# Where three context projections run during an attention block: all after the last heads, or spread behind the groups of heads

## The chip, the cores and the metric

One core of one Trainium2 chip runs the whole program in one launch. The metric is device microseconds (us) of that core for one execution, the median of several runs. TensorE (PE) multiplies, VectorE (DVE) and ScalarE (ACT) do elementwise work, GpSimd (POOL) does a few masks, and SyncE (SP) issues every DMA.

## What is computed

The reference is a chain of two blocks over 256 tokens of width 1024. Block 1 has two layers: in layer 0 a SwiGLU network, an attention mixer and a second SwiGLU network; in layer 1 the same with an RWKV-7 mixer. Block 2 attends over the tokens and a second sequence, the context. What bears on the change is the end of layer 0's mixer, and the projections of the context that block 2 needs.

```python
# block 1, layer 0: four stick-breaking heads, and three groups of four dilated heads
outs, lses = [], []
for g, (window, dilation) in enumerate(DIL_PATTERNS):
    o, l = dilated_window_attention(q[:, :, sl], k[:, :, sl], v[:, :, sl], ...)
    outs.append(o); lses.append(l)
alpha = jax.nn.softmax(jnp.stack(lses, axis=0), axis=0)
out_b = jnp.sum(alpha[..., None] * jnp.stack(outs, axis=0), axis=0)
merged = jnp.concatenate([out_a, out_b], axis=-1)
return merged @ w_out

# block 2, layer 0: one projection of the normalized context, cut in sections
z = h @ p['w_in']
z_glu, z_qa, z_kva, z_kr, z_gq, z_gk, z_gv, z_gate = split_sections(z)
y = a * jax.nn.sigmoid(g)                         # a, g: the halves of z_glu
gates = jax.nn.sigmoid(z_gate + p['b_gate'])
```

The three groups' outputs are weighted with a softmax over the groups, so nothing of `out_b` can be weighted before the third group has its denominators. The context's sections depend on the context alone, so they can be computed at any time before block 2.

## The kernel before

**Products.** Each float32 weight chunk of 512 KB (two 128-row pieces of 512 columns) is loaded (`wraw`, 4 buffers), rounded on ACT to `whi` (L73, 3 buffers), and DVE writes the remainder `wlo` (L74, 3 buffers). A product is then three matmuls: high by high, high by low, low by high. `lin` (L89) streams 512 weight columns past the tokens' 128-column pieces: 12 matmuls a chunk, lines L85, L86, L87. `linT` and `linT_units` (L104, L133) hold the weights and stream 256 tokens: 24 matmuls a chunk, lines L151, L152, L153. Results land in the PSUM buffers `mm`, of which there are three.

**The mixer.** `attn_` (L443) projects and runs the stick-breaking heads, then loops over the three groups g of dilated heads: a projection of values for groups 1 and 2 once, a projection of q and k (`lin`, 4 chunks, two `mm` buffers), and `dil_heads` (L574). That normalizes q and k (squares L579, sums L580, a chain of small DVE operations to L584, the scaling L588), transposes them (L592), and for two token tiles and two parities forms logits (L610), adds the bias (L612), takes the maximum (L614), the exponential with its sum (L618), transposes it (L623) and multiplies by the values (L629). The maxima and sums `md` are transposed (L635) and copied into `stat` (L639, L641).

**The combination.** Behind the loop stand the maximum over groups (L490, L491), a difference and an exponential (L493, L494), products and sums (L496 to L498), a reciprocal (L499), the weights `e` (L500), six transposes of them (L504), their copy `wg` (L506), and for each group and token tile the weighting of `og` (L511), two transposes (L514) and a copy or addition into `ob` (L518, L520). `split` (L449) rounds `ob` to `mh` (L450) and writes the remainder `ml` (L451); then the output projection `w_aout` runs (`lin` at L526), and per half of the columns its result is added to x (L529), which is transposed for the next network (`late_half`, L227 to L231).

**Context steps.** The context was normalized earlier. A generator (`ctx_steps`, L1773) yields its projections one by one; `ctx_ahead(n)` (L1762) runs n of them. The order is in `CO`; the first three are the two halves of the glu section and the first half of gate 0:

```python
CO = [('glu', 0, i) for i in range(2)] + [('gate', br, i) for br in (0, 1, 2) for i in range(2)] + ...
```

Each of the three is 4 chunks by 24 matmuls (96) and two `mm` buffers; ACT and DVE turn the result into `keep` (tanh L1802 and product L1803 for glu, four tanh L1798 for a gate), and SP stores it (L1804, L1799). The calls in the mixer, whose counts the change sets:

```python
        for g in range(3):
            ...
            og.append(s.dil_heads(g, ps, vg, stat, fill))
            ...
            s.ctx_ahead(CE[g])
        ...
        split(ob, 2, 2)
        fill(FA[3])
        s.ctx_ahead(CE[3])
        mf = ...
        for cg in range(2):
            ps = s.lin(wout, cg, mf)
```

**What sets the order.** The framework's scheduler lays down one fixed order per engine when the program is built: an operation that is ready goes ahead of a waiting one, and among ready ones the one written earlier goes first. So a step that is written behind group g starts in the gaps of group g and of what follows it. On the chip each engine takes its own list in order.

Of the kernel before, what the change touches and what calls it, by code (L numbers as in the profile page):

```python
# [360 lines left out]

CE = (0,0,0,3)
FA = (0,(0,0,0),0,0)


class Attn:
# [74 lines left out]
    def attn_(s, x, hi, lo, fill, post, win, wout):  # L443
# [31 lines left out]
        for g in range(3):  # L475
# [8 lines left out]
            if SB == g + 1:  # L484
                s.sb_heads(qT, kT, v, split, fill)
            s.ctx_ahead(CE[g])

# [34 lines left out]
        fill(FA[3])  # L522
        s.ctx_ahead(CE[3])
        mf = [lambda k, t=t: (mh[:, k, t * P:(t + 1) * P], ml[:, k, t * P:(t + 1) * P]) for t in range(2)]
# [1721 lines left out]
```

## Time and profile before

| | |
|---|---|
| median of 3 runs | 2669.93 us (2665.99 to 2678.96) |
| the profiled execution | 2672.3 us, of which its span is 2670.6 us |
| busy share of the span | PE 96%, weight loads 85%, DVE 77%, ACT 52%, POOL 1% |
| mean granted TensorE clock | 0.983 of full speed |
| DMA | 482.35 MB, 181 GB/s |

The mixer's groups lie between 268 and 345 us of the span, the combination between 344 and 364 us, the output projection up to 380 us. In the rows, PE is the matmuls and PEld the weight loads, which overlap them; a time in brackets is how long an engine was idle before the row, and behind the arrow is what ended that. A matmul's own duration is longer than the distance to the next one, since matmuls are pipelined: the start-to-start distance is what one costs.

### The profile page before, as it was taken

The page shows a single profiled execution, that of the slowest core. Times are in us where ns is not written, and L with a number is a line of the kernel's source. Part 1 is how long each engine was busy: PE and PEld are TensorE (multiplying, and loading weights), DVE is VectorE, ACT ScalarE, POOL GpSimd, SP SyncE. Part 2 cuts the span into 40 slices and gives each one's busy share as a digit, 9 for nine tenths or more (in the row PEclk, how much of TensorE's full clock was granted, in tenths as well). Part 3 has the DMA queues.
Part 4 walks back from the last instruction along what each step waited for, and adds up shares of the span by engine and source line. Part 5 has one row for each costly group of instructions (what it writes and reads, how often), then busy time and mean ns, then how long its engine had stood idle before and what let it go on. Part 6 is the DMA issues. An engine that isn't in the chain of part 4 may idle for free.

```text
span 2670.6 us, 49859 instructions
## 1 busy us (share of the span) xinstructions
PE 2574.6 (96%) x20144; PEld 2265.3 (85%) x20144; DVE 2045.9 (77%) x3371; ACT 1387.4 (52%) x2155; POOL 27.7 (1%) x22
## 2 busy tenths in 40 slices
PE   8999999999988999999989999979999999999999
PEld 8986799999865787798876999867979978889997
DVE  7965689679987744796574888789887856997885
ACT  4455554444435323444466565566566645755663
POOL 0000000000001100000000000000000000000000
PEclk9998999999999999999989999989999999999999
DMA  7765368667655355577554565540545555325554
GB/s 262 254 220 164 126 221 270 203 232 248 222 190 195 111 162 170 193 258 230 187 174 142 181 193 183 180 136 25 172 152 179 182 158 170 123 76 174 171 185 152
DMA packets 153136, 482.35 MB, mean 181 GB/s; under 512 B 23709, under 2 KB 38817, under 8 KB 151881
## 3 DMA queue, kind: packets, MB, share of 16 engines
q1 hardware_dynamic: 152906, 479.17, 54.9%
q8 instruction: 158, 2.59, 0.4%
q14 instruction: 72, 0.59, 0.1%
HBM read 466.61 MB, written 12.49 MB: 179 GB/s over the span
## 4 chain that ended last, share of the span: by engine, by line
PE 81%; DVE 10%; ACT 3%; DMA 3%; issue 3%; SPq 0%; POOL 0%; DVEq 0%; ACTq 0%
PE mm L153 9%; PE mm L151 8%; PE mm L152 8%; PE mm L86 8%; PE mm L87 8%; PE mm L85 8%; PE tp L151 6%; PE tp L153 5%; PE tp L152 5%; DVE wlo L74 3%; PE at L1709 2%; PE at L1720 2%; PE tp L1716 1%; DMA mraw<-in_w_modT 1%; PE mm L755 1%
## 5 line engine op out<-in xcount | busy, mean ns | idle before, releaser
L73 ACT CAST whi<-wraw 128x1024 fp32r<-128x1024 f32 (+1 forms) x742 | 770.2, 1040 | 828.3 <-PE mm L87 303.4
L74 DVE TENSOR_TENSOR wlo<-wraw,whi 128x1024 fp32r<-128x1024 f32 (+1 forms) x742 | 897.2, 1211 | 368.9 <-ACT whi L73 359.5
L153 PE MATMUL mm<-hhi,wlo 128*128 128x256 f32 x1872 | 533.1, 286 | 9.9 <-DVE wlo L74 9.7
L151 PE MATMUL mm<-hhi,whi 128*128 128x256 f32 x1872 | 535.0, 286 | 4.8 <-ACT whi L73 2.3
L152 PE MATMUL mm<-hlo,whi 128*128 128x256 f32 x1872 | 532.2, 285 | 0.0
L151 PE MATMUL tp<-hhi,whi 128*128 128x256 f32 x1360 | 390.4, 287 | 0.6 <-ACT R L324 0.2
L153 PE MATMUL tp<-hhi,wlo 128*128 128x256 f32 x1360 | 383.6, 282 | 0.4 <-issue 0.4
L152 PE MATMUL tp<-hlo,whi 128*128 128x256 f32 x1360 | 383.7, 282 | 0.0
L153 PEld LDWEIGHTS mm<-hhi,wlo 128*128 128x128 f32 x1872 | 355.3, 190 | 17.0 <-DVE wlo L74 13.8
L151 PEld LDWEIGHTS mm<-hhi,whi 128*128 128x128 f32 x1872 | 356.9, 191 | 8.2 <-ACT whi L73 3.2
L152 PEld LDWEIGHTS mm<-hlo,whi 128*128 128x128 f32 x1872 | 356.7, 191 | 3.8 <-issue 2.5
L151 PEld LDWEIGHTS tp<-hhi,whi 128*128 128x128 f32 x1360 | 257.8, 190 | 4.6 <-issue 1.3
L153 PEld LDWEIGHTS tp<-hhi,wlo 128*128 128x128 f32 x1360 | 257.7, 190 | 0.6 <-issue 0.6
L152 PEld LDWEIGHTS tp<-hlo,whi 128*128 128x128 f32 x1360 | 257.6, 189 | 0.0
L85 PE MATMUL mm<-whi,fh 128*128 128x512 f32 x616 | 243.2, 395 | 0.7 <-ACT fh L1905 0.5
L86 PE MATMUL mm<-wlo,fh 128*128 128x512 f32 x616 | 242.8, 395 | 0.8 <-DVE wlo L74 0.8
L87 PE MATMUL mm<-whi,fl 128*128 128x512 f32 x616 | 242.8, 395 | 0.0
L86 PE MATMUL mm<-wlo,hhi 128*128 128x512 f32 (+1 forms) x448 | 183.9, 411 | 8.2 <-DVE wlo L74 8.1
L85 PE MATMUL mm<-whi,hhi 128*128 128x512 f32 (+1 forms) x448 | 182.0, 409 | 6.7 <-ACT whi L73 6.7
L87 PE MATMUL mm<-whi,hlo 128*128 128x512 f32 (+1 forms) x448 | 184.4, 412 | 1.8 <-DVE hlo L812 1.8
L1309 DVE CUSTOM_DVE_ANT_0 mjunk<-mraw,crow 128x1024 f32<-128x1024 f32 x112 | 136.8, 1221 | 8.3 <-DMA mraw<-in_w_modT 8.1
L85 PEld LDWEIGHTS mm<-whi,fh 128*128 128x128 f32 x616 | 116.6, 189 | 29.3 <-ACT fh L1905 1.7
(537 smaller groups left out, 3916.0 us busy)
## 6 DMA issues: line engine op xcount, KB each, us to landing
wraw<-in_wgu SPq DMA_DIRECT2D x176, 512.0 KB
wraw<-in_w_up SPq DMA_DIRECT2D x132, 512.0 KB
wraw<-in_w_in SPq DMA_DIRECT2D x124, 512.0 KB
wraw<-in_wd SPq DMA_DIRECT2D x88, 512.0 KB
wraw<-in_w_down SPq DMA_DIRECT2D x66, 512.0 KB
mraw<-in_w_modT SPq DMA_DIRECT2D x64, 512.0 KB
wraw<-in_w_mod SPq DMA_DIRECT2D x32, 512.0 KB
wraw<-in_w_attn SPq DMA_DIRECT2D x24, 512.0 KB
```

Of the source, the lines that this page charges most:

```text
L73: a = nc.scalar.copy(out=hi, in_=raw)
L74: v = nc.vector.tensor_tensor(out=lo, in0=raw, in1=hi, op=ALU.subtract)
L85: s.pinned(mm(ps, lhsT=xh, rhs=wh, start=start, stop=False), pin)
L86: mm(ps, lhsT=xh, rhs=wl, start=False, stop=False)
L87: mm(ps, lhsT=xl, rhs=wh, start=False, stop=stop)
L151: s.pinned(mm(ps, lhsT=wh, rhs=xh, start=start, stop=False), pin)
L152: mm(ps, lhsT=wh, rhs=xl, start=False, stop=False)
L153: mm(ps, lhsT=wl, rhs=xh, start=False, stop=stop)
L755: ins = s.nc.tensor.matmul(*a, **k)
L1309: V.tensor_tensor_reduce(out=t, in0=raw, in1=s.crow[:, c], scale=1.0, scalar=0.0, op0=ALU.mult, op1=ALU.add, accum_out=m[:, k, c:c + 1])
L1709: T.matmul(lg[:, j * S:(j + 1) * S], lhsT=q(hs[par])[:, t * P:(t + 1) * P], rhs=k, start=i == 0, stop=i == len(ks) - 1)
L1720: T.matmul(o[64 * par:64 * par + 64, pr], lhsT=kvs[j // 2][1](4 * g + 2 * pr + par, j % 2), rhs=pTs[par][:, j], start=j == 0, stop=j == nt ...
```

## The change

```diff
-CE = (0,0,0,3)
+CE = (1,1,0,1)
```

`CE[g]` is the number of context steps that are called behind group g, and `CE[3]` the number called behind the combination, ahead of the output projection. Before, all three steps stand at the end. After, the first half of glu stands behind group 0, the second behind group 1, and the half gate alone at the end. No instruction is added or removed: PE has 15,170 rows in the listing of its order on both sides.

The first place is PE in group 0 of the dilated heads, at the two batches of transposes of the normalized q and k (L592) and the first logits (L610). The minus rows belong to the projection of the values of groups 1 and 2 (`lin`), the plus rows to the first glu step.

```order
 L592 MATMUL tp<-ident,qk 128x128 x4
-L85 MATMUL mm<-whi,hhi 128x512
+L151 MATMUL mm<-hhi,whi 128x256
+L152 MATMUL mm<-hlo,whi 128x256
 L592 MATMUL tp<-ident,qk 128x128 x4
-L86 MATMUL mm<-wlo,hhi 128x512
-L87 MATMUL mm<-whi,hlo 128x512
+L153 MATMUL mm<-hhi,wlo 128x256
+L151 MATMUL mm<-hhi,whi 128x256
+L152 MATMUL mm<-hlo,whi 128x256
+L153 MATMUL mm<-hhi,wlo 128x256
 L610 MATMUL at<-kT,qT 128x128 x2
```

The gaps of the heads are filled on both sides: with three matmuls of 512 columns before, with six of 256 columns after. The values' projection moves behind the step, and with it the two projections of q and k that follow.

The second place is PE around the transposes of the group weights (L504). Before, the third step's matmuls stand ahead of them and behind them:

```order
L153 MATMUL mm<-hhi,wlo 128x256
L151 MATMUL mm<-hhi,whi 128x256
L504 MATMUL tp<-ident,e 128x4 x6
L152 MATMUL mm<-hlo,whi 128x256
L153 MATMUL mm<-hhi,wlo 128x256
```

After, from the last group's last logits to the output projection:

```order
L623 MATMUL tp<-ident,L 128x128 x2
L635 MATMUL tp<-ident,md 4x128
L629 MATMUL at<-v_3086,pT 128x64 x2
L504 MATMUL tp<-ident,e 128x4 x6
L514 MATMUL tp<-ident,og 128x128 x12
L85 MATMUL mm<-whi,mh 128x512
L86 MATMUL mm<-wlo,mh 128x512
```

Before, 140 matmuls of the steps stand between the last L635 and the first matmul of the output projection. After, none does: the last step's 96 are laid into the third group, and 18 of the output projection's 48 matmuls (those that need only the stick-breaking heads) stand ahead of the last L635.

The third place is DVE in the combination, from the copies of the maxima and sums on; the minus rows were there before only.

```order
 L639 COPY stat<-tp 4x2x128 x2
 L491 TENSOR_TENSOR M<-M,stat 4x256
-L74 TENSOR_TENSOR wlo<-wraw,whi 128x1024
 L493 TENSOR_TENSOR e<-stat,M 4x768
-L74 TENSOR_TENSOR wlo<-wraw,whi 128x1024
 L496 TENSOR_TENSOR f<-e,stat 4x768
 L497 TENSOR_TENSOR M<-f 4x256
 L498 TENSOR_TENSOR M<-M,f 4x256
-L74 TENSOR_TENSOR wlo<-wraw,whi 128x1024
 L499 RECIPROCAL M<-M 4x256
-L1803 SCALAR_TENSOR_TENSOR keep<-keep,mm 128x512
 L500 TENSOR_TENSOR e<-e,M 4x768
```

The conversions of the steps' weights and the second `keep` are gone from between the combination's operations.

## Rows read from the trace of the kernel before

**Rows 1.** The page: the chain that ended last, by engine, and the two conversions.

```profile
PE 81%; DVE 10%; ACT 3%; DMA 3%; issue 3%; SPq 0%; POOL 0%; DVEq 0%; ACTq 0%
L73 ACT CAST whi<-wraw 128x1024 fp32r<-128x1024 f32 (+1 forms) x742 | 770.2, 1040 | 828.3 <-PE mm L87 303.4
```

**Rows 2.** Busy time by stretch (busy us and instructions): group 0 of heads, then the combination.

```profile
core 0: us, PE busy (x) PEld busy (x) DVE busy (x) ACT busy (x) POOL busy (x), PEclk, DMA share, GB/s
268.00:305.90 37.90, 36.64 (x180) 28.20 (x179) 25.76 (x53) 18.30 (x36) 0.00 (x0) 1.00 0.38 126
...
345.40:363.70 18.30, 18.27 (x153) 17.91 (x153) 16.63 (x33) 7.70 (x10) 0.00 (x0) 1.00 0.48 155
```

**Rows 3.** Timeline of PE in groups 0 and 1: start, duration, line, idle before.

```profile
297.18 0.39 PE L85 MATMUL mm<-whi,hhi 128*128 128x512 f32 x1
297.41 0.39 PE L86 MATMUL mm<-wlo,hhi 128*128 128x512 f32 x1
...
305.93 0.63 PE L592 MATMUL tp<-ident,qk 128*128 128x128 f32 x4 [0.61 <-DVE qk L588]
```

**Rows 4.** Timeline of PE in the combination.

```profile
344.02 0.38 PE L635 MATMUL tp<-ident,md 128*4 128x128 f32 x2
...
346.00 0.28 PE L151 MATMUL mm<-hhi,whi 128*128 128x256 f32 x1
346.12 0.28 PE L152 MATMUL mm<-hlo,whi 128*128 128x256 f32 x1
...
355.70 0.76 PE L504 MATMUL tp<-ident,e 4*128 4x4 f32 x6
...
363.71 0.39 PE L85 MATMUL mm<-whi,mh 128*128 128x512 f32 x1
```

**Rows 5.** Timeline of DVE in the combination.

```profile
344.44 0.74 DVE L639 COPY stat<-tp 4x256 f32<-4x256 f32 x2 [0.47 <-PE tp L635]
345.11 0.40 DVE L491 TENSOR_TENSOR M<-M,stat 4x256 f32<-4x256 f32 x1
...
346.58 0.94 DVE L493 TENSOR_TENSOR e<-stat,M 4x768 f32<-4x768 f32 x1
...
350.39 0.41 DVE L497 TENSOR_TENSOR M<-f 4x256 f32<-4x256 f32 x1
...
352.31 1.73 DVE L499 RECIPROCAL M<-M 4x256 f32<-4x256 f32 x1
...
354.52 0.93 DVE L500 TENSOR_TENSOR e<-e,M 4x768 f32<-4x768 f32 x1
...
361.73 1.22 DVE L74 TENSOR_TENSOR wlo<-wraw,whi 128x1024 fp32r<-128x1024 f32 x1
362.86 0.48 DVE L520 TENSOR_TENSOR ob<-tp,ob 128x128 f32<-128x128 f32 x2
```

**Rows 6.** Timeline of ACT in the combination.

```profile
348.14 0.84 ACT L494 ACTIVATE e<-e 4x768 f32<-4x768 f32 x1
...
364.75 0.61 ACT L450 CAST mh<-ob 128x512 fp32r<-128x512 f32 x1
```

**Rows 7.** Another idle stretch of PE, in layer 1: its timeline.

```profile
762.57 1.17 PE L85 MATMUL mm<-whi,hhi 128*128 128x512 f32 x2 [3.77 <-ACT whi L73]
768.21 0.80 PE L86 MATMUL mm<-wlo,hhi 128*128 128x512 f32 x1 [4.48 <-DVE wlo L74]
768.81 0.63 PE L87 MATMUL mm<-whi,hlo 128*128 128x512 f32 x1
769.23 0.63 PE L85 MATMUL mm<-whi,hhi 128*128 128x512 f32 x1
...
772.65 0.51 PE L85 MATMUL mm<-whi,hhi 128*128 128x512 f32 x1
```

**Rows 8.** Busy time by stretch, same columns as rows 2, inside that idle stretch.

```profile
760.00:762.00 2.00, 0.00 (x0) 0.00 (x0) 1.88 (x6) 1.42 (x3) 0.00 (x0) 1.00 0.87 352
764.00:766.00 2.00, 0.00 (x0) 0.00 (x0) 2.00 (x6) 0.34 (x1) 0.00 (x0) 0.50 0.93 369
```

## The prediction

> **What bounds the kernel now.** The first view is the chain of work that ended last: TensorE holds 81% of it [rows 1]. So the question is not how much work there is, which the change leaves alone, but whether PE is left without work anywhere. The second view is the busy time by stretch: from group 0 of the heads on, PE is busy 36.64 of 37.90 us, and in the combination 18.27 of 18.30 us, at the full granted clock [rows 2]. Since busy time hides how tightly matmuls follow each other, the third view is PE's timeline. In group 0's gaps, matmuls of 512 columns start 0.23 us apart [rows 3]; in the combination, those of 256 columns start 0.12 us apart, more exactly 0.118 on average over a run of them [rows 4]. Both are back to back. The gaps of the heads are thus closed already, by the projections that come next; the combination is closed by the context steps. The fourth view, DVE's timeline of the combination, shows why it needs them: one operation waits for the other from the copies at 344.44 to the last addition at 362.86 [rows 5].
>
> **The change part by part.** The moved steps cost PE the same wherever they stand: 2 x 96 matmuls by 0.118 us = 22.7 us. Behind groups 0 and 1 they push the projections back by that much and take over their role as filler. The rows of the order show the gaps filled one for one, so the time there is worth nothing: 0 us gained. The projections fill the next gaps in turn, and so the shortage arrives at the end. There, 140 step matmuls stood between the last L635 and the output projection, 140 x 0.118 = 16.5 us. None is left, and the 18 early matmuls of the output projection stand ahead of that point too.
>
> What the end takes without filler is the length of the chain. Part one runs from the last L635 to the weights' transposes L504. From L635 at 344.02 to L491 at 345.11 is 1.1 us [rows 4, 5]. Then come L491 0.40, L493 0.94, the exponential 0.84 [rows 5, 6], L496 as long as L493, 0.94, L497 and L498 0.41 each, L499 1.73, L500 0.93 [rows 5]: 6.6 us; nine handovers at some 0.04 us, as from the end of L635 at 344.40 to L639 at 344.44 [rows 4, 5], 0.4. Sum 8.1 us, against the 11.7 us that it took between 344.02 and 355.70 [rows 4], because the weight conversions that stood in between are gone. Part two runs from L504 at 355.70 to the end of the last addition, 362.86 + 0.48 = 363.34; less the conversion of 1.22 us at 361.73 that stood in it [rows 4, 5], 6.4 us. Then the rounding of `ob`, 0.61 us [rows 6], and a handover. The sum is 8.1 + 6.4 + 0.7 = 15.2 us. In it PE has work of its own: before, 363.71 - 344.02 = 19.7 us held 16.5 us of steps, so 3.2 us. **PE stands idle 15.2 - 3.2 = 12.0 us.** Its bounds: 8.2 us if a quarter of the 15.2 us overlapped, which their dependence speaks against, and 16.5 us if the chain took the 19.7 us that it took before.
>
> **Waits in the third group.** Before, groups 0 and 1 each left PE idle for some 0.6 us ahead of their transposes [rows 3], and group 2 did not, since its projection was ready early. Now its projection ends just ahead, and the wait comes a third time: 0.6 us. Its last exponentials stand behind a conversion of 1.04 us on ACT [rows 1]; that is between 0 and 1.04 us, and I take 0.6, since 12 filler matmuls of 0.23 us stand beside it. Together 1.2 us.
>
> **The clock.** In layer 1, PE stands idle from 758.80 to 768.21 but for two matmuls [rows 7]. The granted clock is still 1.00 (2.4 GHz) from 760 to 762, and 0.50 (1.2 GHz) from 764 to 766 [rows 8]. After the restart, 512-column matmuls start 0.42 to 0.43 us apart until 772.65: ten starts in 4.44 us [rows 7], where 0.23 us each would make 2.3 [rows 3]. That is 2.1 us, and I take it for the restart behind the combination, whose 15.2 us hold only 3.2 us of PE work. The transposes L504 and L514 fall into the slow time: 0.6 us, an estimate from the same doubling of some 1.2 us of their work. Bounds: 0 if the clock holds, 4.8 us if it stays low twice as long behind the restart. Taken: 2.7 us.
>
> A rule speaks to the same point. The Trainium skill (Perfetto Trace Analysis, Matmul Optimizations) says that TensorE's power follows its use, and that matmuls should therefore be issued back to back in batches. The trace of layer 1 agrees, with 10 matmuls at 0.43 us behind its gap.
>
> **Queues and buffers.** Each glu step also brings an ACT tanh, a DVE product and a store to its new place. SP takes its list in order, so the weight loads behind a store wait until `keep` is written. DMA engines are 38% busy in group 0 [rows 2] and four chunks are loaded ahead, so I put this at 0; without that cover each of the two stores could hold one chunk, 12 x 0.23 = 2.8 us, or 5.6 us in all. The three `mm` buffers are passed on as they were between projections: 0. Nothing behind the attention is reordered in a way that costs PE.
>
> **Sum.** 12.0 + 1.2 + 2.7 = 15.9, say 16 us. Against the profiled execution, 2672.3 becomes 2688.3 us. That execution lies 2.4 us above the median of the runs, so for a median I say 2669.9 + 16 = **2686 us**.
>
> **Rivals.**
> - *The clock holds.* The transposes L504 and L514 break the idle time in two, and the granted clock may never fall. For it: the two breaks. Against it: in layer 1 two lone matmuls did not keep the clock up [rows 7, 8]. It gives 16 - 2.7 = 13 us, 2683 us, right at the edge of what can be told.
> - *Not slower: the heads had room.* If the matmuls in group 0's gaps are limited by something else than streaming, the steps slip in for nothing there. It would take place from 268 to 306: weight loads fill 28.20 of 37.90 us, so up to 9.7 us of the steps could vanish, and the end would need less of the work it loses. It gives 2669.9 - 9.7 = 2660 us. It decides from the point at which the start-to-start distance in the gaps exceeds 0.23 us; rows 3 show 0.23, which is what it is everywhere in the dense stretches. The Trainium skill (Perfetto Trace Analysis, Identifying the Most-Contended Engine) has a rule that would say so: judge TensorE's headroom by the weight loads' share, not by its busy time. By that share there is 26% of headroom in group 0 and 2% in the combination.
> - *A late restart.* The next network's first chunks are converted behind the combination instead of inside it. If two of them come late, PE waits for two roundings of 1.04 us and two remainders of 1.22 us more [rows 1, 5], 4.5 us: 2690.5 us. Against it: 30 matmuls of the output projection lie between.
> - *The chain is shorter than added up*, at its lower bound of 8.2 us idle, with no waits and no clock loss: 2678 us.
>
> That the change does nothing is excluded by the order of PE, where the step matmuls are gone from the end.
>
> **How the numbers follow.** The forecast has 0.58, the clock that holds 0.15, the late restart 0.14, the shorter chain 0.06, room in the heads 0.07. About 0.5%, 13.3 us, is what a measurement of this kernel can tell from no change. Slower by more: nine tenths of the forecast's case less what the runs' spread of several us takes away from a middle that lies 2.7 us above the edge, a third of the case in which the clock holds, and the late restart: 0.45 + 0.05 + 0.13 = 0.63. Within: the rest of these, the shorter chain and nearly all of the room, 0.34. Faster: 0.03. The range runs from 2675 us, below the shorter chain's value by a few us of spread, to 2696 us, the late restart with the 5.6 us of held loads; it leaves out the room in the heads and little else.
>
> **What would show it.** In the profile after: the stretches of groups 0 and 1 as long as their matmuls ask for, with 256-column matmuls 0.12 us apart in the gaps; between the last L635 and the first matmul of the output projection about 15 us with some 12 us of PE idle, ended by L500, L511 and L450; a granted clock of 0.50 at the end of it and some ten matmuls at 0.43 us behind; everything after shifted by 14 to 18 us. The prediction is wrong if that stretch holds less than 8 us of idle, if the clock stays at 1.00, or if the heads' stretch gets shorter than the work moved into and out of it explains.

## The result, and the profile after

| | before | after |
|---|---|---|
| median | 2670.72 us (2665.85 to 2678.96, 9 runs) | 2685.99 us (2682.55 to 2693.96, 9 runs) |
| ratio | | 1.0061, 95% interval 1.0048 to 1.0074 |
| the profiled execution, its span | 2672.3 us, 2670.6 us | 2682.97 us, 2681.3 us |

The changed kernel is 15.3 us slower, against a forecast of 16; the interval is 12.8 to 19.8 us. In its profile nothing about the amount of work has changed: PE has 20,144 matmuls on both sides and is busy 96% of the span as before, DVE 76%, ACT 52%, and the conversion L73 still takes 1040 ns each [rows 1]. (The page's chain that ended last covers only a third of the span this time, so its shares aren't compared.) What has changed is one place. Here is PE's timeline of the changed kernel from the end of the third group to the output projection: start, duration, line, tiles, count, and in brackets how long PE was idle before and what ended that.

```profile
343.40 0.30 PE L592 MATMUL tp<-ident,qk 128*128 128x128 f32 x1 [0.58 <-DVE qk L588]
...
361.54 0.27 PE L635 MATMUL tp<-ident,md 128*4 128x128 f32 x1
362.16 0.66 PE L629 MATMUL at<-v,pT 128*128 128x64 f32 x4 [0.35 <-ACT pT L625]
369.55 0.81 PE L504 MATMUL tp<-ident,e 4*128 4x4 f32 x6 [6.73 <-DVE e L500]
371.18 1.09 PE L514 MATMUL tp<-ident,og 128*128 128x128 f32 x4 [0.82 <-DVE og L511]
372.49 1.42 PE L514 MATMUL tp<-ident,og 128*128 128x128 f32 x4 [0.22 <-DVE ob L518]
374.10 0.69 PE L514 MATMUL tp<-ident,og 128*128 128x128 f32 x2 [0.19 <-DVE og L511]
375.70 0.69 PE L514 MATMUL tp<-ident,og 128*128 128x128 f32 x2 [0.91 <-DVE og L511]
377.62 0.80 PE L85 MATMUL mm<-whi,mh 128*128 128x512 f32 x1 [1.23 <-ACT mh L450]
378.21 0.63 PE L86 MATMUL mm<-wlo,mh 128*128 128x512 f32 x1
378.64 0.63 PE L85 MATMUL mm<-whi,mh 128*128 128x512 f32 x1
...
380.77 0.89 PE L87 MATMUL mm<-whi,ml 128*128 128x512 f32 x2
381.50 0.39 PE L85 MATMUL mm<-whi,mh 128*128 128x512 f32 x1
```

Between the last L635 and the first matmul behind the roundings there is little but waits: 0.35 + 6.73 + 0.82 + 0.22 + 0.19 + 0.91 + 1.23 = 10.45 us of listed idle time in 16.1 us. Before, that stretch had no listed wait, with step matmuls 0.12 us apart [rows 4]. DVE's and ACT's timelines show why: the links follow each other within some 0.04 us, and PE is the one that waits.

```profile
361.85 0.74 DVE L639 COPY stat<-tp 4x256 f32<-4x256 f32 x2
362.52 0.40 DVE L491 TENSOR_TENSOR M<-M,stat 4x256 f32<-4x256 f32 x1
362.95 0.95 DVE L493 TENSOR_TENSOR e<-stat,M 4x768 f32<-4x768 f32 x1
364.81 0.95 DVE L496 TENSOR_TENSOR f<-e,stat 4x768 f32<-4x768 f32 x1 [0.91 <-ACT e L494]
...
366.69 1.74 DVE L499 RECIPROCAL M<-M 4x256 f32<-4x256 f32 x1
368.46 0.94 DVE L500 TENSOR_TENSOR e<-e,M 4x768 f32<-4x768 f32 x1
```

```profile
363.93 0.84 ACT L494 ACTIVATE e<-e 4x768 f32<-4x768 f32 x1 [0.71 <-DVE e L493]
376.94 0.62 ACT L450 CAST mh<-ob 128x512 fp32r<-128x512 f32 x1 [12.17 <-DVE ob L520]
```

The durations are those of before [rows 5, 6]; what is gone is the weight conversion that stood among them. The busy time by stretch of the changed kernel (the columns of rows 2) gives the clock: 1.00 ahead of the hole, 0.50 at its end, 1.00 again behind the restart.

```profile
359.00:361.00 2.00, 2.00 (x10) 1.09 (x9) 1.45 (x4) 1.51 (x4) 0.00 (x0) 1.00 0.27 43
364.00:366.00 2.00, 0.00 (x0) 0.00 (x0) 1.16 (x2) 0.78 (x1) 0.00 (x0) 0.56 0.28 113
376.00:378.00 2.00, 0.77 (x3) 0.39 (x2) 0.89 (x3) 0.62 (x1) 0.00 (x0) 0.50 0.00 0
382.00:384.00 2.00, 2.00 (x14) 1.52 (x13) 0.96 (x3) 1.84 (x4) 0.00 (x0) 1.00 0.00 0
```

**Where the time went.** Totals of this kernel scatter by over 10 us, so I compare one stretch in the profiles: from the first L592 of group 0 to the first matmul of the next network (L151 behind the output projection). It holds the same work in both kernels, but for one exchange at its start: in after, 36 step matmuls (4.2 us) stand ahead of it, and the 18 of 512 columns that they pushed (4.2 us) in it. I call it *the stretch*: 273.29 to 375.80 us before, 268.10 to 387.54 us after, that is 102.5 against 119.4 us, **16.9 us longer**. Its parts:

- From the first L592 to the last L635 (before: 344.13 us, the second of the two in the row at 344.02): 70.8 us before, 93.4 after, 22.6 more. The 140 step matmuls from the end (16.5 us at 0.118; for 36 of them, the 18 of that exchange stand in this part) and 18 of the output projection (4.2 us at 0.233) came in, 20.7 us; 1.9 us are lost, 0.9 of them in listed waits.
- From the last L635 to the roundings: 19.6 us before, 16.1 after. Without its 16.5 us of steps, PE's own work there was 3.1 us before and is the same now, so 13.0 us are lost.
- From there to the network: 12.1 us before with 48 matmuls of the output projection, 9.9 after with 30. The 18 that are missing are worth 4.2 us and only 2.2 us were saved: 2.0 us are lost, the half clock.

Each of these comes from one profile. How far that can be trusted shows in the first part, which other kernels below have in the same order: it took 70.8 to 70.9 us in four (before, runs 3, 6 and 11) and 93.4 to 93.6 us in four (after, runs 2, 5 and 8). The clock's part is less steady, by about 1 us in run 5.

The profiled executions differ by only 10.7 us in total, less than the stretch and less than the medians. The difference lies ahead of the change, where both kernels execute the same instructions. There the clock stood at half in the profile of before, and not in that of after; first of before, then of after:

```profile
216.00:228.00 12.00, 12.00 (x41) 7.84 (x40) 2.73 (x8) 3.20 (x10) 0.00 (x0) 0.57 0.43 144
256.00:262.00 6.00, 5.25 (x16) 4.08 (x16) 4.41 (x7) 4.26 (x5) 2.15 (x4) 0.72 0.36 107
```

```profile
216.00:228.00 12.00, 12.00 (x59) 8.72 (x59) 3.95 (x9) 4.35 (x12) 0.00 (x0) 1.00 0.55 175
256.00:262.00 6.00, 5.79 (x31) 3.20 (x30) 3.17 (x5) 2.89 (x6) 2.76 (x4) 1.00 0.48 151
```

That is why after reaches its first L592 5.2 us earlier. It isn't a gift of the change: of the eleven experiments below, six have this low clock in their profile and five don't, with the same instructions there. So: -5.2 + 16.9 + 1.6 in the network behind + some -2.6 spread over the other 2100 us = 10.7 us.

### The profile page after: what moved, and what is told of

Same layout as the page of the kernel before. It is cut to its first block, busy times and chain, and to the rows that moved or that the text cites. A ratio compares the mean times of both kernels' runs of the same rounds, so it can differ in the third digit from the quotient of the medians.

```text
span 2681.3 us, 49861 instructions
## 1 busy us (share of the span) xinstructions
PE 2575.0 (96%) x20144; PEld 2264.4 (84%) x20144; DVE 2046.0 (76%) x3371; ACT 1386.2 (52%) x2155; POOL 27.7 (1%) x22
## 5 line engine op out<-in xcount | busy, mean ns | idle before, releaser
L73 ACT CAST whi<-wraw 128x1024 fp32r<-128x1024 f32 (+1 forms) x742 | 769.4, 1040 | 807.6 <-PE mm L87 310.4
L74 DVE TENSOR_TENSOR wlo<-wraw,whi 128x1024 fp32r<-128x1024 f32 (+1 forms) x742 | 896.1, 1210 | 370.7 <-ACT whi L73 359.7
L151 PE MATMUL mm<-hhi,whi 128*128 128x256 f32 x1872 | 535.7, 286 | 5.1 <-ACT whi L73 2.5
L151 PE MATMUL tp<-hhi,whi 128*128 128x256 f32 x1360 | 390.0, 287 | 0.5 <-ACT R L324 0.2
L151 PEld LDWEIGHTS mm<-hhi,whi 128*128 128x128 f32 x1872 | 357.5, 191 | 9.0 <-ACT whi L73 3.4
L151 PEld LDWEIGHTS tp<-hhi,whi 128*128 128x128 f32 x1360 | 257.6, 189 | 4.4 <-issue 1.0
```

Source lines behind the costliest of these rows:

```text
L73: a = nc.scalar.copy(out=hi, in_=raw)
L74: v = nc.vector.tensor_tensor(out=lo, in0=raw, in1=hi, op=ALU.subtract)
L151: s.pinned(mm(ps, lhsT=wh, rhs=xh, start=start, stop=False), pin)
```

## The experiments

Theory A: the time is lost where PE runs out of work at the end, because the chain there is bare. Theory B, the rival: a step costs by standing behind a group of heads (more waits, more buffers, more queues), whatever is left at the end. The size of the clock's part is a question of its own.

**1. One step behind group 0, two at the end.**

```diff
-CE = (1,1,0,1)
+CE = (1,0,0,2)
```

> One step behind the first group of heads, two at the end. Theory A (the time is lost only where PE runs out of work in the combination): in PE's order 58 step matmuls and 14 of the output projection now stand between the last L635 and L504, 6.8 + 3.3 = 10 us, which covers part one of the chain (8.1 us); 4 of the output projection, 0.9 us, and PE's own 2.3 us are all that stands in part two (7.1 us). So 3.9 us idle there and next to none in part one; with up to 1 us of waits in the groups +4 to +5 us against before, 2675 to 2676 us, and the granted clock stays at 1.00 or falls for a microsecond or two only. Theory B (a step costs by standing behind a group of heads, 15.3 / 2 each, whatever is left at the end): +7.6 us, 2678 us, with the loss in the heads' stretch and not in the combination. The places of the idle time tell them apart better than the total.

Measured: 2678.06 us, ratio to before 1.0021 (1.0009 to 1.0034), that is +5.6 us. The stretch is 108.9 us, +6.3. Its waits are where A put them: none ahead of L504, and the rest in part two.

```profile
360.26 0.73 PE L504 MATMUL tp<-ident,e 4*128 4x4 f32 x6
...
361.95 0.62 PE L514 MATMUL tp<-ident,og 128*128 128x128 f32 x4
362.98 0.44 PE L514 MATMUL tp<-ident,og 128*128 128x128 f32 x2 [0.41 <-DVE ob L518]
364.33 0.77 PE L514 MATMUL tp<-ident,og 128*128 128x128 f32 x4 [0.92 <-DVE og L511]
365.40 0.44 PE L514 MATMUL tp<-ident,og 128*128 128x128 f32 x2 [0.30 <-DVE ob L520]
367.07 0.50 PE L85 MATMUL mm<-whi,mh 128*128 128x512 f32 x1 [1.23 <-ACT mh L450]
...
367.87 0.39 PE L86 MATMUL mm<-wlo,mh 128*128 128x512 f32 x1
368.10 0.57 PE L85 MATMUL mm<-whi,mh 128*128 128x512 f32 x1
368.47 0.63 PE L87 MATMUL mm<-whi,ml 128*128 128x512 f32 x1
```

2.86 us of waits, where 3.9 were expected. But the clock cost more than expected: it fell when the output projection was already running, and from 368.10 us on eight starts in a row are 0.37 to 0.43 us apart, some 1.5 us. The total alone can't tell A from B here; the places speak for A.

**2 and 3. The hole filled again, with the two steps left behind the heads.** Run 2 and its partner, run 3, which takes the same five steps early but all at the end:

```diff
-CE = (1,1,0,1)
+CE = (1,1,0,3)
```

```diff
-CE = (0,0,0,3)
+CE = (0,0,0,5)
```

> The two steps of the change stay behind the first two groups, and three steps, the fourth and fifth of the list among them, stand at the end, so that the end has its full filler again (more than 110 step matmuls behind the last L635). Theory A: the combination has no idle time and the clock stays at 1.00 there; the time is that of five steps at the end (the next run) within 2 us. Theory B: it is slower than that run by 15 us, as after is slower than before.

> None behind the heads, five steps at the end: the partner of the run before, with the same work taken early. Both theories: the combination as in the kernel before, no idle time. What the two additional steps, 2 x 11.3 = 22.7 us of PE ahead of the network, give back behind it is not known from the attention: all of it where they were executed at the cost of PE's time later, nothing if they stood in gaps there. So between 0 and +22.7 us against before; my estimate is +5 us.

Measured: 2684.84 us, 1.0038 (1.0024 to 1.0053), and 2681.97 us, 1.0036 (1.0022 to 1.0049). The stretches are 126.9 and 125.2 us (both with 22.7 us of additional steps): the two steps behind the heads cost **1.8 us**, of which 1.0 in listed waits, and not 15. (The medians are 2.9 us apart, for 2 expected; their scatter is larger than that.) From the last L635 to the output projection run 2 has no listed wait, and its clock over the combination is 1.00:

```profile
366.00:388.00 22.00, 21.90 (x183) 21.42 (x184) 19.36 (x36) 11.08 (x19) 0.00 (x0) 1.00 0.49 163
```

So B is out. Of the 22.7 us that two more steps take early, run 3 keeps 9.6 us as a loss (2672.9 x 0.0036); in its profile, where it lags the kernel before by 20 us at 889 us, it gets back some 10 us by 1247 us, behind the place where those steps stood. On the way the lag first grows to 28.7 us, at 991 us; it grows there in run 6 too, which moves no step (last section). So filling the hole with further work isn't shown to be free, and its own price stays open.

**4. The clock alone: the hole filled with matmuls of no use.**

```diff
-        s.ctx_ahead(CE[3])
+        s.ctx_ahead(CE[3])     # one line in the kernel, broken here
+        ps = s.pm.tile([P, 2, S], F32, name="mm", tag="mm")
+        for i in range(90):
+            nc.tensor.matmul(ps[:, i % 2], lhsT=s.act0.hi[:, i % 8, :P], rhs=s.act0.hi[:, i % 8], start=True, stop=True)
```

> The changed kernel with 90 additional matmuls of 128x256 over the context's activations, whose result is not used, behind the last step: in PE's order 37 of them stand in the third group in place of 18 matmuls of the output projection, and 53 behind the last L635, followed by those 18. Nothing useful is added. Theory A with the clock as predicted: the chain still takes 15 to 16 us from the last L635 to the first roundings of the second half, the granted clock stays at 1.00, the matmuls behind it start 0.23 us apart from the first: the loss shrinks by the clock's share alone, 2.0 to 2.7 us against after, 2683 to 2684 us. If the clock is the larger part of the loss: 5 us or more less than after, 2681 us or below. If idle time does not bring the clock down: no change against after in the spacing.

Measured: 2690.47 us, 1.0058 (1.0044 to 1.0072); the stretch 119.2 us, 0.25 less than after. The chain took 16.5 us to the first matmul behind the roundings, where 15 to 16 were expected, and listed idle time fell from 10.45 to 2.20 us. But the clock did fall, later:

```profile
374.81 0.44 PE L514 MATMUL tp<-ident,og 128*128 128x128 f32 x2 [0.45 <-DVE og L511]
376.99 0.65 PE L85 MATMUL mm<-whi,mh 128*128 128x512 f32 x1 [1.75 <-ACT mh L450]
...
380.74 0.39 PE L85 MATMUL mm<-whi,mh 128*128 128x512 f32 x1
```

```profile
374.00:376.00 2.00, 0.80 (x4) 0.20 (x2) 2.00 (x5) 0.00 (x0) 0.00 (x0) 1.00 0.02 4
376.00:378.00 2.00, 1.01 (x3) 0.82 (x4) 0.98 (x3) 0.62 (x1) 0.00 (x0) 0.80 0.51 166
378.00:380.00 2.00, 2.00 (x6) 1.53 (x5) 0.00 (x0) 0.00 (x0) 0.00 (x0) 0.50 0.24 96
```

The filler had run out ahead of the last rounding. Two waits, of 0.45 and 1.75 us, were enough for nine matmuls in 3.75 us, where after, behind 10 us of waits, has nine in 3.88. A miss, and the reason for run 7.

**7. The last wait filled too.** In addition to run 4, 14 such matmuls into a `tp` tile behind the loop over the groups, ahead of `split(ob, 2, 2)`.

> The changed kernel with the 90 additional matmuls of the fourth run and 14 more, 1.65 us, behind the last L514, where PE still waited 1.75 us for the rounding there and the granted clock fell to 0.50 from about 377 to 380.7 us. If that last wait brings the clock down: it now stays at 1.00, the matmuls of the output projection start 0.23 us apart from the first, eight of them 0.2 us sooner each, and the stretch from the first L592 to the network falls from 119.2 to 117.5 us. If the clock falls for what happened further ahead: again eight matmuls at 0.43 us, and 119.2 us.

Measured: the stretch 117.7 us, 1.45 us less than in run 4, with the clock at 1.00 throughout and the first nine matmuls in 2.20 us, to 385.27:

```profile
380.89 0.44 PE L514 MATMUL tp<-ident,og 128*128 128x128 f32 x2 [0.44 <-DVE og L511]
381.08 1.91 PE L521 MATMUL tp<-hhi 128*128 128x256 f32 x14
383.07 0.50 PE L85 MATMUL mm<-whi,mh 128*128 128x512 f32 x1
383.41 0.39 PE L86 MATMUL mm<-wlo,mh 128*128 128x512 f32 x1
383.64 0.39 PE L85 MATMUL mm<-whi,mh 128*128 128x512 f32 x1
```

```profile
382.00:384.00 2.00, 1.92 (x13) 1.59 (x12) 1.06 (x3) 0.62 (x1) 0.00 (x0) 1.00 0.52 162
```

So in these profiles it is the wait for the rounding that brings the clock down, and the clock's part of the loss is about 1.7 us (119.4 to 117.7). The chain is as long as ever, 16.5 us. In total the kernel is no faster: 2690.69 us, 1.0074 (1.0056 to 1.0091). Its profile loses what it gained, and more, between 889 and 1110 us: its lag behind the kernel before grows there from 17.6 to 31.8 us (run 4: 13.9 to 19.0 us, after: not at all). The last section comes back to that.

**5 and 6. One more link in the chain, in after and in before.**

```diff
-        nc.vector.reciprocal(out=M, in_=M)
+        [nc.vector.reciprocal(out=M, in_=M) for _ in range(2)]
```

> The changed kernel with the reciprocal L499 done twice on M, one more link of 1.74 us in part one of the chain (the values of the second half's heads are then no longer the reference's). Theory A (PE waits for the chain): the stretch from the first L592 to the network's first matmul grows by 1.8 us, from 119.4 to 121.2 us, and the wait ahead of L504 from 6.7 to 8.5 us; the time is 1.8 us above after. If something else than the chain ends the stretch: 119.4 us and no change.

> The same additional reciprocal in the kernel before. PE's order then has 114 step matmuls between the last L635 and L504, 13.4 us, against 8.1 + 1.8 = 9.9 us of chain, and 26 with 10 of the output projection behind. Theory A: covered, the stretch stays at 102.5 us within 0.5 us and the time at that of before. If the chain already ends the stretch in the kernel before: +1.8 us, as in the run above.

Measured in after: 2692.1 us, 1.0079 (1.0057 to 1.0101); the stretch 122.3 us, +2.8. The wait ahead of L504 grew by just the link, from 6.73 to 8.50 us, and the other 1.1 us are the clock's, which rose later behind the restart (389.24 us is still 0.43 behind 388.82):

```profile
376.33 0.80 PE L504 MATMUL tp<-ident,e 4*128 4x4 f32 x6 [8.50 <-DVE e L500]
...
388.82 0.63 PE L86 MATMUL mm<-wlo,mh 128*128 128x512 f32 x1
389.24 0.63 PE L87 MATMUL mm<-whi,ml 128*128 128x512 f32 x1
```

Measured in before: 2674.42 us, 1.0005 (0.9992 to 1.0018); the stretch 103.3 us, +0.8, with no listed wait at all between the last L635 and the output projection. That is 0.3 us more than I had allowed, and I can't place it; the link's 1.74 us don't show. The link is bare in after and covered in before.

**8 and 11. A shorter chain, in after and in before.** The weights are divided behind the transposes, where they lie on 128 partitions:

```diff
-        nc.vector.reciprocal(out=M, in_=M)
-        nc.vector.tensor_tensor(out=e, in0=e, in1=M[:, None].to_broadcast([4, 3, S]), op=ALU.mult)
...
                 nc.tensor.transpose(out=wps[:, g, t], in_=s.perm(e[:, g], g, t), identity=s.ident[:4, :4])
+                nc.tensor.transpose(out=wms[:, g, t], in_=s.perm(M, g, t), identity=s.ident[:4, :4])
...
-        nc.vector.tensor_copy(out=w, in_=wps)
+        nc.vector.reciprocal(out=w, in_=wms)
+        nc.vector.tensor_tensor(out=w, in0=w, in1=wps, op=ALU.mult)
```

> The changed kernel with the division moved behind the transposes: L499 (1.74 us) and L500 (0.94 us) on 4 partitions are left out, M is transposed as e is (six more transposes of 4x4 blocks), and a reciprocal and a product of 24 columns on 128 partitions take the place of the copy L506, each 0.2 us by that row. Theory A: the chain loses 2.7 us and gains some 0.5 us, the stretch falls from 119.4 to 117.2 us and the time by 2.2 us. If the chain doesn't end the stretch: 119.4 us.

> The shorter chain of the eighth run in the kernel before. Theory A: in the kernel before, the three steps cover the chain, so a shorter one is worth nothing: stretch 102.5 us plus at most 0.6 us for six more transposes, and the time of before within 1 us. If the chain already ends the stretch in the kernel before: 2.2 us less, as the eighth run gained on after.

Measured in after: the stretch 116.8 us, 2.6 us less, and the end 13.3 instead of 16.1 us. (L505 are the new transposes; from here on this kernel's lines are two higher, so L516 is L514 of the others.)

```profile
364.78 0.76 PE L504 MATMUL tp<-ident,e 4*128 4x4 f32 x6 [2.01 <-ACT e L494]
366.74 0.81 PE L505 MATMUL tp<-ident,M 4*128 4x4 f32 x6 [1.20 <-DVE M L498]
368.71 1.09 PE L516 MATMUL tp<-ident,og 128*128 128x128 f32 x4 [1.16 <-DVE og L513]
```

Up to the first transposes of `og`, 6.73 + 0.82 us of waits have become 2.01 + 1.20 + 1.16. The total, 2687.11 us, 1.0067 (1.005 to 1.0084), doesn't resolve 2.6 us from after. Measured in before: the stretch 103.3 us, +0.8, total 2674.43 us, 1.001 (0.9996 to 1.0024): nothing gained, and six transposes paid for, at 0.2 us more than expected.

**9 and 10. Can a step be moved for nothing, or at a gain?** Both have the shorter chain, one step moved and two at the end. In run 9 it stands behind group 0, `CE = (1,0,0,2)`; in run 10 in the stick-breaking heads, ahead of a wait that PE has in before, with `CE = (0,0,0,2)` and

```diff
-            fill(FA[0])
+            s.ctx_ahead(j)
```

> The shorter chain of the eighth run in the kernel with one step behind the first group and two at the end. Theory A: the end takes what is longer, the chain, 13.3 us from the last L635 to the output projection in the eighth run, or PE's work there, 55 step matmuls, 13 of the output projection and PE's own 3.2 us, 6.5 + 3.0 + 3.2 = 12.7 us; nearly equal, so that about 1 us is lost with the handovers, where the first run lost 6.3 us. The stretch from the first L592 to the network: 103.5 to 104.5 us (102.5 before, 108.9 in the first run), the clock at 1.00, the time 1 to 2 us above before. If the step behind the heads costs by itself: some 108 us as in the first run.

> As the run before, but the one step stands in the stick-breaking heads, ahead of their second half, where PE waited 2.38 us for POOL ahead of L561 in the profile of before (at 256.75 us) and the clock fell to 0.50 behind it. PE's order has 69 of its matmuls there, 8.1 us, where 22 of 512 columns and the wait took 7.5 us. Theory A (steps are worth what idle time they fill): 1.8 to 2.4 us gained there, 1 us lost at the end; from the first L542 to the network 132.1 us before become 131 us, or 129.5 us where the clock doesn't fall at L561; the time 0 to 2.5 us below before, 2668 to 2671 us. If the steps delay the heads' chain there: no gain, 2672 us.

Run 9: 2674.37 us, 1.0013 (0.9997 to 1.0028); the stretch 105.5 us. It loses 3.0 us against before, where run 1 lost 6.3: the right direction, 1 us more than expected. 0.8 us is the price of six transposes, as in run 11, and 0.8 us more in listed waits; the rest I can't place. The clock stays at 1.00. Run 10: 2672.07 us, 1.0008 (0.9993 to 1.0024), from the first L542 to the network 133.8 us. A miss by 3 us: PE waited there all the same, now for ACT, which is busy with those heads and rounds the steps' weights late: three chunks in a row, from 257.56 us.

```profile
258.64 0.39 PE L151 MATMUL mm<-hhi,whi 128*128 128x256 f32 x1 [1.82 <-ACT whi L73]
```

Neither beats the kernel before.

## Why the prediction was right

The forecast's mechanism holds, and its sum, 15.9 us, was made against one profiled execution. Against that, the stretch measures 16.9 us. Closer than its terms is the median: 2686 us were forecast and 2685.99 measured, and that is luck. With 1.6 us in the network behind, which the sum put at 0, the terms make 18.5 us in the profiles, and the interval of the medians' difference, 12.8 to 19.8 us, doesn't tell 16 from 18.5.

- **The heads' gaps are filled one for one, 0 us gained.** Right. Of the 9.7 us of room that the share of the weight loads would give, nothing showed: 20.7 us of matmuls came in and 22.6 us of time. The spacing of 0.23 us [rows 3] was the better guide than that share. The Trainium skill (Perfetto Trace Analysis, Identifying the Most-Contended Engine) judges TensorE's headroom by MFU, the share of its peak rate, or by the weight loads' share; the second misleads here, with 26% of room by rows 2 and none in the runs, and the first was not worked out.
- **Waits in the third group, 1.2 us.** Its third wait for L588 came, 0.58 us for 0.6; the wait at its tail is 0.35 us, for 0.6. Two small ones that I hadn't listed (0.22 and 0.18 us ahead of L623, on L618) and 1.0 us between instructions bring the groups' loss to 1.9 us. Runs 2 and 3 give the same cost by another way, 1.8 us.
- **The chain, 15.2 us.** It took 16.1. Part one is 361.54 to 369.55, 8.0 us for 8.1. Part two is 8.1 us for 6.4 + 0.7: its transposes L514 ran at half clock, four in 1.09 us where the kernel of run 1 shows 0.62. With the 0.6 us that I had set aside for that under the clock, 12.6 us were predicted and 13.0 measured. Two small slips are in the sum: it counts nine handovers in part one, where L491 to L504 has eight (0.04 us), and it takes off the whole conversion of 1.22 us, though the addition behind it starts 0.09 us before its listed end [rows 5]. Runs 5 and 8 show that this time is the chain's: a link of 1.74 us more is 1.77 us of wait more, two links of 2.7 us less make the stretch 2.6 us shorter, and in before neither counts.
- **The clock at the restart, 2.1 us.** 2.0 us by the stretch's parts, and 1.7 us by run 7; in run 5 it took 1.1 us more. I had taken ten slow starts and got nine. The reason I gave was too narrow, though: I tied the fall to an idle time as long as the one in layer 1. Runs 1 and 4 show it behind waits of 1 to 2 us.
- **Queues and buffers, 0.** Nearly: SP waited 2.8 us in all for `keep` ahead of the two glu stores, and no listed wait of PE follows from it; from the network's first matmul to its first L227 behind it (532 us in before) it took 157.8 us, where before took 156.2. That 1.6 us is all there is of the late restart that I had priced at 4.5 us, and one wait of 0.24 us for L74 is all that is listed of it.

The step that failed is in what was to show it: "everything after shifted by 14 to 18 us". In the profile the shift is 11.7 us at the network's first matmul and 10.7 at the end. The sum took the profiled execution of before as a base, and that one had lost 5.2 us to the clock ahead of the change, in a place where the next execution may not. Between the medians, which average over this, the difference is 15.3 us, and between the fastest runs 2682.55 - 2665.85 = 16.7 us.

The rivals: the clock that holds fell with the rows of after; room in the heads fell with the stretch; the late restart came to a third of its price; the shorter chain would have needed waits below 8.2 us, and 10.45 are listed alone.

## What to carry to other kernels

Filler is worth what is idle where it stands, so before moving it, ask of both ends: is the gap it goes to already closed (look at the distance between starts, not at the busy share), and how long is the chain that it leaves bare. Here the old place held 16.5 us of filler over a chain that needs about 13, and the new places were full. If filler must leave, shorten the chain first: with the division moved behind the transposes, one step could leave for 3.0 instead of 6.3 us. And where effects are under 1%, compare the same stretch in two profiles beside the totals: the stretch told runs apart by 1 to 3 us, when totals of one kernel scatter by 10.

## What the runs showed of the hardware

- **Small waits can bring the clock down, and longer ones need not.** Behind 0.45 and 1.75 us of idle time (run 4) the granted clock went from 1.00 to 0.50 and eight matmuls of 512 columns ran at 0.43 us; in run 1, with single waits of 0.30 to 1.23 us, it fell when matmuls had already been running at 0.23 us for a microsecond. Where the longest wait at the end was 0.44 or 0.55 us (runs 7, 9, 10) it stayed at 1.00. But the wait's length alone doesn't decide. Ahead of L561 PE waits 2.38 us in before and in after:

```profile
256.75 1.40 PE L561 MATMUL tp<-sp,ones 128*128 128x256 f32 x4 [2.38 <-POOL sp L550]
```

```profile
252.88 1.13 PE L561 MATMUL tp<-sp,ones 128*128 128x256 f32 x4 [2.38 <-POOL sp L550]
```

  The first is before: the clock falls to 0.50 behind the wait, as in runs 2, 5, 7, 9 and 11. The second is after: the clock is 1.00 from 252 to 262 us, as it is behind this wait in runs 1, 3, 4, 6 and 8. So one profile each, as in runs 4 and 7, shows what a wait did there, and not what it will do each time. The Trainium skill (Perfetto Trace Analysis, Matmul Optimizations) asks for matmuls back to back in batches; runs 4 and 7 agree, and put about 1.5 us on the last gap alone.
- **The same instructions meet different clocks.** From 216 to 228 us, in the kernels with the same instructions up to there, the mean clock is 0.57 to 0.63 in seven profiles (before, runs 2, 5, 7, 9, 10 and 11, with 34 to 43 matmuls in 12 us) and 1.00 in the other six (after, runs 1, 3, 4, 6 and 8, with 59 or 60). This place alone, with its sequel at 256 us, is worth 5.2 us between before and after. The totals go with the clock: of 29 executions of before beside runs 9 to 11, the two at a mean clock of 0.981 took 2682 and 2683 us, and the five at 0.987 took 2663 to 2669. What decides it stays open.
- **Waits that end with nothing the profile shows.** The 2048 matmuls of 32x32 at L979 (L981 in runs 8 to 11), far behind the change, wait for "issue" 1.8 us in before and 1.6 us in after, but 4.1 us in run 6, whose only addition is one reciprocal 600 us earlier, 4.9 us in run 4, about 5.5 in runs 2 and 3, and 7.1 us in run 7, where the clock is also 0.57 from 912 to 928 us. Between 889 and 1110 us the lag behind before grows by 8 us in run 6, by 5 in run 4 and by 14 in run 7. So it isn't tied to the useless matmuls. In their profiles it hides what runs 4 and 7 gained in the stretch; whether it does so in their medians isn't shown. It wasn't followed further.
